# Two token tiles at a time between the layers, and key transposes one step later

## The chip, the cores and the metric

The kernel runs on one core of a Trainium2 chip. The metric is the device time of one execution in microseconds; lower is better. The kernel before takes 1199.09 us, the median of 3 runs (1197.3 to 1199.76).

## What is computed

Two layers of a hybrid encoder work on 512 tokens of 1024 features. Each layer makes one large input projection of the modulated input u, feeds two attention mixers with it, merges them through gates, projects back, adds the residual and normalises. The output of the first layer's normalisation is the second layer's input.

```
def hybrid_layer(x, c, ...):
    mod = jax.nn.silu(c) @ w_ada + b_ada
    shift, scale, gate = jnp.split(mod, 3, axis=-1)
    u = x * (1.0 + scale[:, None, :]) + shift[:, None, :]
    proj = u @ w_in
    aq, ak, av, az, bq, bk, bv, bz, gl = jnp.split(proj, SPLIT_POINTS, axis=-1)
    y_a = mixer_a(aq, ak, av, rel_table) * jax.nn.silu(az)
    y_b = mixer_b(bq, bk, bv, q_norm_g, k_norm_g) * jax.nn.silu(bz)
    g_a, g_b = jnp.split(jax.nn.sigmoid(gl + b_gate), 2, axis=-1)
    merged = g_a * (y_a @ w_pa) + g_b * (y_b @ w_pb)
    out = merged @ w_o
    return layer_norm(DEEPNORM_ALPHA * x + gate[:, None, :] * out, ln_g, ln_b)
```

Mixer B normalises queries and keys per head by their root mean square and rotates them before the scores; it uses 8 query heads (`bq`) and 2 key and value heads (`bk`, `bv`).

## The kernel before

**Number format.** Every large product is made of three TensorE products: each operand is held as a rounded high part and a low part, the difference. For u these are `uh` and `ul`, for weights `wh` and `wl` (or tiles `g` where the weights are kept longer). A weight chunk of 1024 x 256 comes in as two raw loads and is split in four pieces of two feature blocks each: ACT copies the high part (line 175), DVE subtracts for the low part (line 176).

**Order.** The order of each engine's instructions is the order in which the code is written out; each engine runs its own instructions in that order and waits on the others through semaphores. The program advances in ticks. `tick(n)` splits n weight pieces and runs what `later(k, f)` has put off by k ticks. With `split_first` the pieces come ahead of what was put off.

**Between the layers.** `out_proj` goes through 16 units, one for each column chunk j of 256 and token tile r of 128; a unit is 24 products of 256 columns, and DVE then empties it with three instructions (gate, residual, statistics; lines 1211, 1213, 1217). The last eight units are chunks 2 and 3 of tile 0, then of tile 1, 2 and 3. After chunk 3 of a tile, `layer_norm` takes the aggregate (line 1236), POOL raises to the power -1/2 (line 1238), and `normalise` refines that on DVE (lines 1244 to 1269) and scales the tile on ACT in two halves (line 1271). `make_u` transposes half a tile, four blocks of 128 x 128, on TensorE (line 944), ACT scales and shifts each block out of PSUM (line 948), makes `uh` (line 952), and DVE makes `ul` (line 953). `normalise` is put off by one tick, the two halves of `make_u` by `LN` = 2 and 3 ticks.

**The first chunks of layer 1.** `first_chunks` computes, for each token tile, one unit of keys and values (`bkv`, into the PSUM tile L) and one of the first queries (`bq0`, into T), and then four units of `bq1`. `FIRST` holds how many weight pieces are split after each unit.

**Steps of mixer B.** `b_steps` is a generator of small steps: rotate the keys, scale them (`k_scale`), take square sums and roots of queries (`q_sums`), transpose the keys (`b_keys`, line 597, copied out at 599 and 600) and rotate queries (`q_rotate`, lines 492 and 501). In layer 0 the last steps, in layer 1 those that are left, are run by `b_prepare`, with one unit of projection work between two of them (`weave`); then `mixer_b` transposes the first queries (line 613), takes their scores into L and their exponentials (line 637). POOL takes the roots of the square sums (line 480). Line 423 copies a row of the bias table out of PSUM.

Of the kernel before, what the change touches and what calls it, by code (L numbers as in the profile page):

```python
# [30 lines left out]
WARM = (6, 6)  # L31
AGE = 2
PIECES = (1, 1, 1, 1, 2, 2, 2, 2, 1, 1, 1, 1, 0, 0, 1, 1)
FIRST = (2, 1, 1, 1, 1, 0, 0, 1)
LN = (2, 3)


@with_exitstack
def trunk_kernel(ctx, tc, x, c, rel_table, ln_g, ln_b, w_ada, b_ada, w_in, b_gate,
# [41 lines left out]
    B1 = Slots(psum, "b", 4, [128, 512])  # L81
# [62 lines left out]
    hi_lo = {}  # L144
# [14 lines left out]
    def drop(key):  # L159
        for w in hi_lo.pop(key):  # L160
            if isinstance(w, Held):
                G.put(*w.tiles)
# [371 lines left out]
    def k_scale(st):  # L534

        v, y, t = (st["kn"][:, j] for j in range(3))
        newton(v, y, t)
        for rp in range(2):
            kd = st["kd", rp] = G.get()
            kdv = kd.rearrange("p (r h e d) -> p r h e d", r=2, h=2, e=2)  # L540
            for r2 in range(2):
                r = 2 * rp + r2
                dve.tensor_tensor(out=kdv[:, r2], in0=st["km"][:, r, :, None, :].to_broadcast([128, 2, 2, 64]),
                                  in1=y[:, 2 * r:2 * r + 2][:, :, None, None].to_broadcast([128, 2, 2, 64]), op=MUL)

    def q_sums(st, ch, rp):
        if "qn" not in st:
            st["qn"] = small.tile([128, 3, 32], F32, tag="qn", name=fresh("qn"))
        at = 16 * ch + 8 * rp
        square_sums(st["xq", ch, rp], st["qn"][:, 0, at:at + 8])  # L550
        first_root(st["qn"][:, 0, at:at + 8], st["qn"][:, 1, at:at + 8])
# [11 lines left out]
    def b_steps(st):  # L563

        k_rotate(st)
        yield
        k_scale(st)
        q_sums(st, 0, 0)
        yield
        b_keys(st)  # L570
        q_rotate(st, 0, 0)
        yield
        q_sums(st, 0, 1)
        q_sums(st, 1, 0)
        yield
        while ("xq", 1, 1) not in st:
            yield
        q_sums(st, 1, 1)
# [358 lines left out]

    xs = dsc.tile([512, 1024], F32, name="xs")

    def make_u(r, h, xn):  # L940

        b = B1.get()
        for k in range(4):
            pe.transpose(b[:, 128 * k:128 * k + 128], xn[:, 128 * k:128 * k + 128], idn)
        u = G.get()
        for k in range(4):
            kt, ks = 4 * h + k, slice(128 * k, 128 * k + 128)
            act.activation(u[:, ks], b[:, ks], AF.Identity, bias=aff[:, kt:kt + 1], scale=aff[:, 8 + kt:9 + kt])  # L948
        B1.put(b)
        uv = u.rearrange("p (k t) -> p k t", k=4)  # L950
        ks, ts = slice(4 * h, 4 * h + 4), slice(128 * r, 128 * r + 128)
        act.activation(uh[:, ks, ts], uv, AF.Copy)
        dve.tensor_sub(ul[:, ks, ts], uv, uh[:, ks, ts].bitcast(F32))
        G.put(u)

    def first_chunks(l, st):

        big_o = {"bkv": big("L"), "bq0": big("T")}

        def unit(n, r):  # L960
            token_mms(hi_lo[l, n], big_o[n][:, 256 * r:256 * r + 256], slice(128 * r, 128 * r + 128))
            if r % 2:
                o = big_o[n].rearrange("p (r n) -> p r n", r=4)[:, r - 1:r + 1]
                if n == "bkv":
                    b_copy_kv(r - 1, 2, o, st)
                else:
                    b_copy_q(0, r // 2, o, st)

        for r in range(4):
            for i, n in enumerate(("bkv", "bq0")):  # L970
                unit(n, r)
                if r == 3:
                    next(st["steps"], None)
                tick(FIRST[2 * r + i], True)
        drop((l, "bkv"))
        drop((l, "bq0"))
        for _ in token_chunk((l, "bq1"), lambda r: slice(128 * r, 128 * r + 128),
                             lambda rp, o: b_copy_q(1, rp, o.rearrange("p (r n) -> p r n", r=2), st)):
            next(st["steps"], None)

    def warm(o, n):

        for _ in range(n):
# [245 lines left out]
        for j in range(4):  # L1229
            drop((l, f"wo{j}"))  # L1230

    def layer_norm(l, r, xt, rows, bn):

        mv = small.tile([128, 6], F32, tag="mv", bufs=4, name=fresh("mv"))
        mean, v, y, t, nb = (mv[:, i:i + 1] for i in (0, 2, 3, 4, 5))
        dve.bn_aggr(mv[:, 0:2], bn.rearrange("p a b -> p (a b)"))
        dve.tensor_scalar(v, mv[:, 1:2], eps, None, op0=ADD)
        pool.tensor_tensor(out=y, in0=v, in1=mhalf, op=OP.pow)

        def put_out(h):  # L1240
            sp.dma_start(dram(out, r * 128 * D + 512 * h, [[D, 128], [1, 512]]), xt[h])

        def rstd():
            dve.scalar_tensor_tensor(t, y, v, y, op0=MUL, op1=MUL)
            dve.tensor_scalar(t, t, -0.5, 1.5, op0=MUL, op1=ADD)
            dve.tensor_mul(y, y, t)

        last = l == DEPTH - 1
        if last:
            def centre():  # L1250
                for h in range(2):
                    dve.scalar_tensor_tensor(xt[h], xt[h], mean, rows[0][h], op0=SUB, op1=MUL)  # L1252
                rstd()

            def finish():
                centre()
                for h in range(2):
                    dve.scalar_tensor_tensor(xt[h], xt[h], y, rows[1][h], op0=MUL, op1=ADD)  # L1258
                    put_out(h)

            if r == 3:
                run_later(True)
                finish()
            else:
                later(1, finish)
            return
        def normalise():
            rstd()
            dve.scalar_tensor_tensor(nb, mean, -1.0, y, op0=MUL, op1=MUL)
            for h in range(2):  # L1270
                act.activation(xt[h], xt[h], AF.Identity, scale=y, bias=nb)  # L1271

        later(1, normalise)
        for h in range(2):
            later(LN[h], lambda h=h: make_u(r, h, xt[h]))


    def row_tiles(src, offs):
# [7 lines left out]
    for l in range(DEPTH):  # L1286
        st = {"more": deque()}
        st["steps"] = b_steps(st)
        if l == 0:
            start_layer0(st)  # L1290
        else:
            todo = deque([(r, h) for r in range(4) for h in range(2)])

            def keep():
                if todo:
                    r, h = todo.popleft()
                    t = nxt[r][h]
                    dve.tensor_mul(t, t, gb[0][h])
                    dve.tensor_add(t, t, gb[1][h])
                    sp.dma_start(xs[128 * r:128 * r + 128, 512 * h:512 * h + 512], t)  # L1300
                    G.put(t)
                    if not todo:
                        G.put(*gb[0], *gb[1])

            first_chunks(l, st)
        yb = {n: G.get() for n in range(4)}
        ya, zs, merged, b_done = {}, {}, {}, {}
        src = x[0] if l == 0 else xs
        xt = {}

        def preload(n):
            for r in range(len(xt), min(len(xt) + n, 4)):
                xt[r] = [G.get(), G.get()]
                for h in range(2):
                    sp.dma_start(xt[r][h], src[128 * r:128 * r + 128, 512 * h:512 * h + 512])

        def main():
            yield from b_prepare(st, deque([keep] * 8 if l else []))
            yield from mixer_b(st, yb)
            b_done["b"] = True  # L1320
            G.put(st["v"], st["ks", 0], st["ks", 1])
            yield from mixer_a(st, 0, ya, deque([lambda: None] * 4 + [lambda: load_bias(st, 1)]))
            yield from mixer_a(st, 1, ya)

        def fill():
            yield from half_chunks(l, st, 0)
            yield from half_chunks(l, st, 1)
            yield from z_chunks(l, zs)
            yield from merge_chunks(l, ya, yb, b_done, zs, merged, preload)

        weave(main(), fill(), RATE)
        if l + 1 < DEPTH:
            rope_loads(l + 1)
            later(2, lambda: rope_tables(l + 1))
            later(1, lambda: affine(l + 1))
        preload(4)
        if l + 1 < DEPTH:
            rows = None
            gb = row_tiles(ln_g[l], [0]) + row_tiles(ln_b[l], [0])
        else:  # L1340
            rows = row_tiles(ln_g[l], [0]) + row_tiles(ln_b[l], [0])
        out_proj(l, merged, xt, lambda r, bn: layer_norm(l, r, xt[r], rows, bn))
        for t in merged.values():
            G.put(*t)
        if l + 1 < DEPTH:
            for hh in range(2):
                gate_tile(l + 1, hh)
        nxt = xt
# [49 lines left out]
```

## Time and profile before

| what | us |
|---|---|
| median of 3 runs | 1199.09 |
| profiled execution | 1199.13 |
| its span | 1197.0 |
| TensorE busy in the span | 1163.0 |
| DVE busy | 675.4 |
| ACT busy | 531.1 |
| POOL busy | 54.0 |

The span is the time from the first to the last instruction of the program that the profiler saw; the execution's own time has a little around it. Busy time is a union: a matmul's record is longer than the distance to the next one, so the start distances, not the lengths, give what a product costs. TensorE is the engine whose share decides; the others matter where TensorE waits for them.

### The profile page before, as it was taken

Reading aid. Unit: us, or ns where it says so; the run is one execution under the profiler, and the core shown is the slowest. Engines: PE = TensorE matmul, PEld = TensorE weight load, DVE = VectorE, ACT = ScalarE, POOL = GpSimd, SP = SyncE. Lnnn points to the kernel's source line nnn. Section 1 sums busy time; section 2 is a strip of 40 time slices with the busy share of each in tenths; the row PEclk is TensorE's granted clock in tenths of the full one; section 3 lists DMA queues with packets and bytes.
Section 4 is the critical chain, followed back from the end, with each engine's and each line's share of the span. In section 5 each row is a group of like instructions: output and inputs, shape, how many; then the busy total and the mean of one; then the engine's idle time right before and its main releaser. Section 6 shows DMA issues by size and latency. Waiting matters only on the chain.

```text
span 1197.0 us, 19187 instructions
## 1 busy us (share of the span) xinstructions
PE 1163.0 (97%) x7491; PEld 998.2 (83%) x7491; DVE 675.4 (56%) x1582; ACT 531.1 (44%) x1112; POOL 54.0 (5%) x85
## 2 busy tenths in 40 slices
PE   7899999999999999999989999999999999999996
PEld 6888888888887787888989888888878778888896
DVE  6776766655455365336755667664333533843477
ACT  2364544444554454323275545544554553533320
POOL 0021000001000000000002001000000000000000
PEclk9999999999999999999999999999999999999998
DMA  9935433546343243334522326335232223323331
GB/s 280 294 116 150 123 109 117 150 133 185 103 128 120 59 129 96 90 104 150 170 71 71 114 91 182 112 107 167 83 114 85 88 73 114 116 88 106 123 107 71
DMA packets 161314, 146.31 MB, mean 122 GB/s; under 512 B 8942, under 2 KB 149078, under 8 KB 161224
## 3 DMA queue, kind: packets, MB, share of 16 engines
q1 hardware_dynamic: 159176, 139.71, 38.5%
q0 software_dynamic: 2048, 5.38, 1.9%
q8 instruction: 59, 0.97, 0.3%
q14 instruction: 31, 0.25, 0.1%
HBM read 134.87 MB, written 8.62 MB: 120 GB/s over the span
## 4 chain that ended last, share of the span: by engine, by line
PE 88%; DVE 6%; ACT 2%; DMA 1%; issue 1%; SPq 1%; POOL 0%; DVEq 0%; ACTq 0%
PE b L90 75%; PE L L90 6%; PE T L663 5%; DVE acc L283 1%; PE T L90 1%; DMA raw<-in_w_ada_dram 1%; PE b L613 1%; DVE wl L176 1%; ACT g L948 0%; DMA s<-in_w_in_dram 0%; SPq L999 0%; DVE g L1252 0%; DVE g L1258 0%; ACT g L1271 0%; DVE wl L1023 0%
## 5 line engine op out<-in xcount | busy, mean ns | idle before, releaser
L176 DVE TENSOR_TENSOR wl<-raw,wh 128x512 fp32r<-128x512 f32 x304 | 205.1, 687 | 286.1 <-ACT wh L175 286.1
L90 PE MATMUL b<-uh,wh 128*128 128x512 f32 x768 | 308.4, 402 | 0.6 <-ACT g L423 0.6
L90 PE MATMUL b<-uh,wl 128*128 128x512 f32 x768 | 299.5, 390 | 1.7 <-DVE wl L176 1.7
L90 PE MATMUL b<-ul,wh 128*128 128x512 f32 x768 | 300.0, 391 | 0.0
L175 ACT ACTIVATE wh<-raw 128x512 fp32r<-128x512 f32 x304 | 179.9, 622 | 32.7 <-issue 24.8
L90 PEld LDWEIGHTS b<-uh,wh 128*128 128x128 f32 x768 | 144.0, 188 | 43.6 <-issue 12.0
L90 PEld LDWEIGHTS b<-uh,wl 128*128 128x128 f32 x768 | 144.2, 188 | 33.8 <-DVE wl L176 2.5
L90 PEld LDWEIGHTS b<-ul,wh 128*128 128x128 f32 x768 | 144.3, 188 | 27.6
L90 PE MATMUL b<-wh,uh 128*128 128x256 f32 x416 | 120.8, 290 | 0.0
L90 PE MATMUL b<-wl,uh 128*128 128x256 f32 x416 | 117.7, 283 | 0.0
L90 PE MATMUL b<-wh,ul 128*128 128x256 f32 x416 | 117.6, 283 | 0.0
L665 ACT ACTIVATE pt<-T 128x1024 f32<-128x1024 f32 x64 | 65.4, 1022 | 73.3 <-PE T L663 70.3
L738 ACT ACTIVATE s<-s,ast 128x256 f32<-128x256 f32 x128 | 63.5, 497 | 68.3 <-DVE ast L733 62.9
L283 DVE SCALAR_TENSOR_TENSOR acc<-raw,sc,acc 128x256 f32<-128x256 f32 x168 | 81.3, 484 | 8.4 <-DMA raw<-in_w_ada_dram 3.2
L90 PEld LDWEIGHTS b<-wh,uh 128*128 128x128 f32 x416 | 79.5, 191 | 4.8 <-issue 3.6
L90 PEld LDWEIGHTS b<-wl,uh 128*128 128x128 f32 x416 | 79.5, 191 | 0.8 <-DVE wl L176 0.2
L90 PEld LDWEIGHTS b<-wh,ul 128*128 128x128 f32 x416 | 79.4, 191 | 0.0
L90 PE MATMUL b<-g,wh 128*128 128x512 f32 x256 | 79.2, 391 | 0.0
L637 ACT ACTIVATE s<-L,bst,qn 128x512 f32<-128x512 f32 x64 | 49.2, 773 | 65.9 <-DVE bst L634 65.9
L90 PE MATMUL b<-wh,g 128*128 128x256 f32 x384 | 71.4, 284 | 0.7 <-DVE g L1191 0.5
L90 PE MATMUL b<-pt,g 128*64 128x128 f32 x1024 | 70.0, 279 | 0.0
L90 PEld LDWEIGHTS b<-pt,g 128*64 128x64 f32 x1024 | 54.6, 136 | 17.7 <-issue 13.7
(177 smaller groups left out, 1615.5 us busy)
## 6 DMA issues: line engine op xcount, KB each, us to landing
raw<-in_w_in_dram SPq DMA_DIRECT2D x126, 512.0 KB, 4.1
raw<-in_w_ada_dram SPq DMA_DIRECT2D x96, 256.0 KB, 3.9
raw<-in_w_o_dram SPq DMA_DIRECT2D x16, 512.0 KB
g<-in_x_dram SPq DMA_DIRECT2D x16, 256.0 KB, 5.5
vph<-g SPq DMA_DIRECT2D x16, 256.0 KB, 2.1
g<-vph SPq DMA_DIRECT2D x16, 256.0 KB, 6.0
g<-frow SPq DMA_DIRECT2D x32, 128.0 KB, 3.1
raw<-in_w_pa_dram SPq DMA_DIRECT2D x8, 512.0 KB, 3.5
```

Source lines behind the costliest of these rows:

```text
L90: pe.matmul(o, l, r, start=start, stop=stop, skip_group_check=True)
L175: act.activation(hi[:, d], raw[:, s], AF.Copy)
L176: dve.tensor_sub(lo[:, d], raw[:, s], hi[:, d].bitcast(F32))
L283: dve.scalar_tensor_tensor(a, raw[:, k], col, a, op0=MUL, op1=ADD)
L613: pe.transpose(o[:, 128 * e:128 * e + 128], qd[:, 2 * (hp % 2) + e], idn)
L637: act.activation(p[:, 512 * e:512 * e + 512], lg[:, 512 * e:512 * e + 512], AF.Exp, scale=f[:, e:e + 1], bias=sm[:, 0, e:e + 1], accum_out ...
L663: pe.transpose(t[:, 128 * j:128 * j + 128], p[:, 128 * j:128 * j + 128], idn)
L665: act.activation(pt, t, AF.Copy)
L738: act.activation(p4[:, e, b], p4[:, e, b], AF.Exp, bias=sm[:, e, b:b + 1], accum_out=s_t[:, rb, e, 1:2])
```

## The change

Four edits. The normalisation of a tile between the layers is issued in the same tick as its statistics, no longer one tick later. `make_u` takes two token tiles and a quarter of the features in place of one tile and half of them: its four transposes are followed by two scaled copies of 256 columns in place of four of 128. Nothing is made until the second tile of a pair is normalised; two of the four pieces are then made two ticks later, and two three ticks later. The first chunks go through tiles 0 and 1 for `bkv`, `bq0` and `bq1` and then through tiles 2 and 3, with another list of weight pieces, and the steps of mixer B advance only after units of tile 3. In `b_steps` scaling the keys and the first square sums are two steps, and the last three square sums are one.

```
--- before.py
+++ after.py
@@ -31,8 +31,9 @@
 WARM = (6, 6)
 AGE = 2
 PIECES = (1, 1, 1, 1, 2, 2, 2, 2, 1, 1, 1, 1, 0, 0, 1, 1)
-FIRST = (2, 1, 1, 1, 1, 0, 0, 1)
-LN = (2, 3)
+FIRST = (("bkv", 0, 2), ("bq0", 0, 1), ("bkv", 1, 1), ("bq0", 1, 2), ("bq1", 0, 0), ("bq1", 1, 0),
+         ("bkv", 2, 0), ("bq0", 2, 0), ("bkv", 3, 1), ("bq0", 3, 2), ("bq1", 2, 1), ("bq1", 3, 1))
+LN = (2, 2, 3, 3)
 
 
 @with_exitstack
@@ -565,6 +566,7 @@
         k_rotate(st)
         yield
         k_scale(st)
+        yield
         q_sums(st, 0, 0)
         yield
         b_keys(st)
@@ -572,7 +574,6 @@
         yield
         q_sums(st, 0, 1)
         q_sums(st, 1, 0)
-        yield
         while ("xq", 1, 1) not in st:
             yield
         q_sums(st, 1, 1)
@@ -937,18 +938,20 @@
 
     xs = dsc.tile([512, 1024], F32, name="xs")
 
-    def make_u(r, h, xn):
+    def make_u(r, j, xt):
 
         b = B1.get()
-        for k in range(4):
-            pe.transpose(b[:, 128 * k:128 * k + 128], xn[:, 128 * k:128 * k + 128], idn)
+        for k in range(2):
+            for i in range(2):
+                c = 128 * (2 * (j % 2) + k)
+                pe.transpose(b[:, 256 * k + 128 * i:256 * k + 128 * i + 128], xt[r + i][j // 2][:, c:c + 128], idn)
         u = G.get()
-        for k in range(4):
-            kt, ks = 4 * h + k, slice(128 * k, 128 * k + 128)
+        for k in range(2):
+            kt, ks = 2 * j + k, slice(256 * k, 256 * k + 256)
             act.activation(u[:, ks], b[:, ks], AF.Identity, bias=aff[:, kt:kt + 1], scale=aff[:, 8 + kt:9 + kt])
         B1.put(b)
-        uv = u.rearrange("p (k t) -> p k t", k=4)
-        ks, ts = slice(4 * h, 4 * h + 4), slice(128 * r, 128 * r + 128)
+        uv = u.rearrange("p (k t) -> p k t", k=2)
+        ks, ts = slice(2 * j, 2 * j + 2), slice(128 * r, 128 * r + 256)
         act.activation(uh[:, ks, ts], uv, AF.Copy)
         dve.tensor_sub(ul[:, ks, ts], uv, uh[:, ks, ts].bitcast(F32))
         G.put(u)
@@ -966,18 +969,26 @@
                 else:
                     b_copy_q(0, r // 2, o, st)
 
-        for r in range(4):
-            for i, n in enumerate(("bkv", "bq0")):
+        o1 = {}
+
+        def last(r):
+            if r % 2 == 0:
+                o1[0] = B1.get()
+            o = o1[0]
+            token_mms(hi_lo[l, "bq1"], o[:, 256 * (r % 2):256 * (r % 2) + 256], slice(128 * r, 128 * r + 128))
+            if r % 2:
+                b_copy_q(1, r // 2, o.rearrange("p (r n) -> p r n", r=2), st)
+                B1.put(o)
+
+        for n, r, k in FIRST:
+            if n == "bq1":
+                last(r)
+            else:
                 unit(n, r)
-                if r == 3:
-                    next(st["steps"], None)
-                tick(FIRST[2 * r + i], True)
-        drop((l, "bkv"))
-        drop((l, "bq0"))
-        for _ in token_chunk((l, "bq1"), lambda r: slice(128 * r, 128 * r + 128),
-                             lambda rp, o: b_copy_q(1, rp, o.rearrange("p (r n) -> p r n", r=2), st)):
-            next(st["steps"], None)
-
+            if r == 3:
+                next(st["steps"], None)
+                drop((l, n))
+            tick(k, True)
     def warm(o, n):
 
         for _ in range(n):
@@ -1229,8 +1240,9 @@
         for j in range(4):
             drop((l, f"wo{j}"))
 
-    def layer_norm(l, r, xt, rows, bn):
-
+    def layer_norm(l, r, tiles, rows, bn):
+
+        xt = tiles[r]
         mv = small.tile([128, 6], F32, tag="mv", bufs=4, name=fresh("mv"))
         mean, v, y, t, nb = (mv[:, i:i + 1] for i in (0, 2, 3, 4, 5))
         dve.bn_aggr(mv[:, 0:2], bn.rearrange("p a b -> p (a b)"))
@@ -1270,9 +1282,10 @@
             for h in range(2):
                 act.activation(xt[h], xt[h], AF.Identity, scale=y, bias=nb)
 
-        later(1, normalise)
-        for h in range(2):
-            later(LN[h], lambda h=h: make_u(r, h, xt[h]))
+        normalise()
+        if r % 2:
+            for j, n in enumerate(LN):
+                later(n, lambda j=j: make_u(r - 1, j, tiles))
 
 
     def row_tiles(src, offs):
@@ -1339,7 +1352,7 @@
             gb = row_tiles(ln_g[l], [0]) + row_tiles(ln_b[l], [0])
         else:
             rows = row_tiles(ln_g[l], [0]) + row_tiles(ln_b[l], [0])
-        out_proj(l, merged, xt, lambda r, bn: layer_norm(l, r, xt[r], rows, bn))
+        out_proj(l, merged, xt, lambda r, bn: layer_norm(l, r, xt, rows, bn))
         for t in merged.values():
             G.put(*t)
         if l + 1 < DEPTH:
```

The order of ACT's instructions between the layers. Line 1271 (1283 after) normalises a tile, 948 and 952 (951 and 955) make u and its high part, 175 (176) copies weight pieces; raw_5515 and raw_5558 are the halves of the `bq0` chunk. Before, from the normalisation of tile 2 on:

```order
L1271 ACTIVATE g_5280<-g_5280,mv_5839 128x512
L1271 ACTIVATE g_5281<-g_5281,mv_5839 128x512
L175 ACTIVATE wh_5872<-raw_5515 128x512
L948 ACTIVATE g_5932<-b_5927,aff 128x128 x4
L952 ACTIVATE uh<-g_5932 128x4x128
L175 ACTIVATE wh_5872<-raw_5558 128x512 x2
L948 ACTIVATE g_5984<-b_5979,aff 128x128 x4
L952 ACTIVATE uh<-g_5984 128x4x128
L1271 ACTIVATE g_5284<-g_5284,mv_5939 128x512
L1271 ACTIVATE g_5285<-g_5285,mv_5939 128x512
```

After, from the same normalisation on:

```order
L1283 ACTIVATE g_5280<-g_5280,mv_5823 128x512
L1283 ACTIVATE g_5281<-g_5281,mv_5823 128x512
L176 ACTIVATE wh_5862<-raw_5515 128x512
L951 ACTIVATE g_5871<-b_5866,aff 128x256 x2
L955 ACTIVATE uh<-g_5871 128x2x256
L951 ACTIVATE g_5881<-b_5876,aff 128x256 x2
L955 ACTIVATE uh<-g_5881 128x2x256
L176 ACTIVATE wh_5862<-raw_5515 128x512
L1283 ACTIVATE g_5284<-g_5284,mv_5919 128x512
L1283 ACTIVATE g_5285<-g_5285,mv_5919 128x512
L176 ACTIVATE wh_5862<-raw_5558 128x512 x2
```

The two pieces of raw_5558 stood ahead of the last normalisation and now stand behind it.

The order of DVE's instructions around the statistics of tile 2 (tile g_5281 is its second half; 1236 and 1248 aggregate; 1211 to 1217 and 1222 to 1228 empty a unit). Before:

```order
L1211 TENSOR_TENSOR wot_5823<-b_5798,gate_631 128x256
L1213 SCALAR_TENSOR_TENSOR g_5281<-g_5281,wot_5823 128x256
L1217 BN_STATS bn_5407<-g_5281 128x6
L953 TENSOR_TENSOR ul<-g_5832,uh 128x4x128
L1236 BN_AGGR mv_5839<-bn_5407 128x2
L1237 TENSOR_SCALAR mv_5839<-mv_5839 128x1
L1211 TENSOR_TENSOR wot_5868<-b_5843,gate_631 128x256
L1213 SCALAR_TENSOR_TENSOR g_5285<-g_5285,wot_5868 128x256
L1217 BN_STATS bn_5439<-g_5285 128x6
```

After:

```order
L1222 TENSOR_TENSOR wot_5799<-b_5774,gate_631 128x256
L1224 SCALAR_TENSOR_TENSOR g_5281<-g_5281,wot_5799 128x256
L1228 BN_STATS bn_5407<-g_5281 128x6
L956 TENSOR_TENSOR ul<-g_5808,uh 128x2x256
L956 TENSOR_TENSOR ul<-g_5818,uh 128x2x256
L1248 BN_AGGR mv_5823<-bn_5407 128x2
L1249 TENSOR_SCALAR mv_5823<-mv_5823 128x1
L1256 SCALAR_TENSOR_TENSOR mv_5823<-mv_5823 128x1
```

Before, the aggregate followed the low part of one piece of tile 1; now it follows those of two pieces of tiles 0 and 1 together.

The order of ACT's instructions in layer 0 from the first key copies (line 599, 600 after) to the first query copies (615, 616). Line 898 (899) copies out a unit of the projection, 475 (476) squares queries, 489 (490) swaps halves for the rotation. Before:

```order
L599 ACTIVATE g_834<-b_829 128x512
L599 ACTIVATE g_842<-b_837 128x512
L489 ACTIVATE s_845<-g_772 128x16x16 x2
L898 ACTIVATE g_878<-b_800 128x512
L175 ACTIVATE wh_825<-raw_623 128x512
L475 ACTIVATE s_885<-g_776 128x512
L475 ACTIVATE s_890<-g_774 128x512
L175 ACTIVATE wh_825<-raw_625 128x512
L475 ACTIVATE s_922<-g_778 128x512
L615 ACTIVATE qst_930<-b_927 128x256
L615 ACTIVATE qst_936<-b_933 128x256
```

After:

```order
L899 ACTIVATE g_853<-b_794 128x512
L176 ACTIVATE wh_819<-raw_623 128x512
L600 ACTIVATE g_865<-b_860 128x512
L600 ACTIVATE g_873<-b_868 128x512
L490 ACTIVATE s_876<-g_772 128x16x16 x2
L176 ACTIVATE wh_819<-raw_625 128x512
L476 ACTIVATE s_912<-g_776 128x512
L476 ACTIVATE s_917<-g_774 128x512
L476 ACTIVATE s_922<-g_778 128x512
L616 ACTIVATE qst_930<-b_927 128x256
L616 ACTIVATE qst_936<-b_933 128x256
```

Before, the copy of a projection unit stands between the key copies and the query copies; now it stands ahead of both, and three squares follow each other.

## Rows read from the trace of the kernel before

**Rows 1.** The page, busy us (share of the span) and instructions by engine.

```profile
PE 1163.0 (97%) x7491; PEld 998.2 (83%) x7491; DVE 675.4 (56%) x1582; ACT 531.1 (44%) x1112; POOL 54.0 (5%) x85
```

**Rows 2.** Groups by shape, TensorE: busy us, mean ns | idle before, releaser.

```profile
L944 PE MATMUL b<-idn,g 128*128 128x128 f32 x32 | 5.1, 282 | 6.0 <-ACT g L1271 6.0
...
L597 PE MATMUL b<-idn,g 128*128 128x128 f32 x16 | 3.5, 299 | 0.3 <-DVE g L543 0.3
```

**Rows 3.** Timeline of TensorE between the layers: start, length, what, idle before.

```profile
592.98 3.04 PE L90 MATMUL b<-g,g 128*128 128x256 f32 x24
596.72 0.66 PE L944 MATMUL b<-idn,g 128*128 128x128 f32 x4 [0.71 <-ACT g L1271]
...
622.47 0.74 PE L944 MATMUL b<-idn,g 128*128 128x128 f32 x4 [1.82 <-ACT g L1271]
...
623.23 0.42 PE L90 MATMUL L<-wl,uh 128*128 128x256 f32 x1
623.44 0.41 PE L90 MATMUL L<-wh,ul 128*128 128x256 f32 x1
```

**Rows 4.** Windows: length, busy of PE, PEld, DVE, ACT, POOL, granted clock, DMA.

```profile
623.00:626.20 3.20, 3.20 (x17) 3.20 (x16) 1.17 (x2) 2.66 (x7) 0.00 (x0) 0.50 0.03 9
```

**Rows 5.** Timeline of ACT between the layers.

```profile
595.86 1.52 ACT L1271 ACTIVATE g<-g,mv 128x512 f32<-128x512 f32 x2 [9.65 <-DVE mv L1269]
...
599.32 0.63 ACT L952 ACTIVATE uh<-g 128x512 fp32r<-128x512 f32 x1
...
616.95 1.14 ACT L175 ACTIVATE wh<-raw 128x512 fp32r<-128x512 f32 x2
...
621.61 1.52 ACT L1271 ACTIVATE g<-g,mv 128x512 f32<-128x512 f32 x2 [1.47 <-DVE mv L1269]
```

**Rows 6.** Timeline of DVE between the layers.

```profile
592.15 0.26 DVE L1236 BATCH_NORM_AGGREGATE mv<-bn 128x2 f32<-128x24 f32 x1
...
595.03 0.21 DVE L1244 SCALAR_TENSOR_TENSOR mv<-mv 128x1 f32<-128x1 f32 x1
...
595.66 0.16 DVE L1269 SCALAR_TENSOR_TENSOR mv<-mv 128x1 f32<-128x1 f32 x1
...
599.98 0.69 DVE L953 TENSOR_TENSOR ul<-g,uh 128x512 fp32r<-128x512 f32 x1 [1.35 <-ACT uh L952]
...
604.24 0.42 DVE L1211 TENSOR_TENSOR wot<-b,gate 128x256 f32<-128x256 f32 x1
...
605.15 0.43 DVE L1217 BATCH_NORM_STATS2 bn<-g 128x6 f32<-128x256 f32 x1
```

**Rows 7.** Timeline of POOL between the layers.

```profile
592.68 0.57 POOL L1238 TENSOR_TENSOR mv<-mv,mhalf 128x1 f32<-128x1 f32 x1 [24.07 <-DVE mv L1237]
```

**Rows 8.** Lines 948 and 1034 alone: duration ns min/median/max, first and last start, forms.

```profile
L948 ACT ACTIVATE g<-b,aff x32: 438/451/482, 597.8 to 629.6; 128x128 f32<-128x128 f32 x32
...
L1034 ACT ACTIVATE g<-b,mod x8: 778/778/783, 12.1 to 56.7; 128x512 f32<-128x512 f32 x8
```

**Rows 9.** Timeline of TensorE in layer 0, keys and first queries.

```profile
68.07 1.77 PE L597 MATMUL b<-idn,g 128*128 128x128 f32 x8 [0.25 <-DVE g L543]
...
75.43 0.60 PE L613 MATMUL b<-idn,g 128*128 128x128 f32 x4
...
87.69 0.50 PE L90 MATMUL b<-uh,wh 128*128 128x512 f32 x1 [0.60 <-ACT g L423]
```

**Rows 10.** Timeline of DVE in layer 0, rotation of the first queries.

```profile
73.11 1.29 DVE L501 TENSOR_TENSOR g<-g,s 128x512 f32<-128x512 f32 x2
```

**Rows 11.** Timeline of POOL in layer 0, roots of the query sums.

```profile
75.88 4.83 POOL L480 TENSOR_TENSOR qn<-qn,mhalf 128x8 f32<-128x8 f32 x3 [3.93 <-DVE qn L479]
```

**Rows 12.** Timeline of TensorE in layer 1, the same transposes.

```profile
645.05 1.74 PE L597 MATMUL b<-idn,g 128*128 128x128 f32 x8
...
655.26 0.60 PE L613 MATMUL b<-idn,g 128*128 128x128 f32 x4
```

**Rows 13.** Timeline of DVE in layer 1, rotation of the first queries.

```profile
650.69 1.29 DVE L501 TENSOR_TENSOR g<-g,s 128x512 f32<-128x512 f32 x2
```

## The prediction, made before the changed kernel ran

> **What bounds the kernel now.** I read the page's busy line first: TensorE is busy for 1163.0 of 1197.0 us [rows 1], so an edit is worth what it does to TensorE's waits or its clock, and nothing else. The groups of TensorE instructions by shape say where it waits: the 32 transposes of line 944, between the layers, lost 6.0 us, all to ACT's normalisation at line 1271, and the 16 key transposes of line 597 a little to DVE [rows 2]. TensorE's timeline shows the first of the four waits between the layers, 0.71 us, and the last, 1.82 us [rows 3]. It also gives the unit of this stage: 24 products of 256 columns, whose starts reach over 3.04 − 0.28 + 0.12 = 2.88 us, 0.120 us each. After the fourth wait the products start 0.21 us apart, and the stretch that follows has a granted clock of 0.50, which is the 1.2 GHz level [rows 3, 4]. About 15 products there take 0.21 instead of 0.12 and the transposes ahead of them stretch too: 1.45 us. Those 7.4 us are all that the boundary can give. I then read ACT, DVE and POOL over the same stretch to see what each wait hangs on [rows 5 to 7].
>
> The profiled execution took 1199.13 us with a span of 1197.0; the median of the runs is 1199.09. I add to the former; the 0.04 between them does not matter.
>
> **Part 1, between the layers: the waits removed.** Normalisation of a token tile used to be queued one unit late, behind another unit's three DVE instructions. At once, it is ready in time for its transposes, which now come two units later. The four waits go: −6.0 us.
>
> **Part 1: what is late next.** I play the new order from the end of the unit of column chunk 3 and tile 1, called (3,1), at 592.98 + 2.88 = 595.9 [rows 3]. TensorE, unhindered: units (2,2) and (3,2) to 601.6; eight transposes of 0.109 (0.87) to 602.5; unit (2,3) to 605.4; eight transposes to 606.2; unit (3,3) to 609.1. Then the first `bkv` unit may start.
>
> ACT must by then have made u for tiles 0 and 1, in four pieces of 512 columns: two scaled copies of 256 columns and one rounding copy (0.63 [rows 5]) each. No row shows the scaled copy at 256 columns; at 128 it takes 0.451 and at 512 0.778 [rows 8], and these are my bounds. I take 0.56, the straight line between them, since both are the same operation from the same memory. The Trainium skill (ScalarE: Activation LUTs, What ACT_TABLE_LOAD costs) gives 0.28 us for a column pointer as bias, 0.09 for the second pointer and 0.833 ns an element, which is an estimate of 0.585; by that the sum would be 0.3 higher. A piece thus costs ACT about 1.5 with overlaps. Pieces 0 and 1 are rounded at 605.2 and DVE has their low parts 0.69 later [rows 6], 605.9.
>
> Only now does DVE reach the statistics of tile 2, which stand behind those low parts. From the aggregate to the normalisation: 0.53 to POOL's root, 0.57 there, 0.79 for the four small DVE instructions, some 0.06 between [rows 6, 7]: 1.95. ACT waits at the normalisation until 607.9, takes 1.52 for its two halves [rows 5], then a weight piece (0.5), then pieces 2 and 3: rounded at 611.5 and 613.0, low parts at 612.2 and 613.7. The `bkv` unit begins at 609.1, does 12 products on pieces 0 and 1, and waits twice; it ends at 614.2 instead of 612.0. **+2.2.**
>
> Tile 3 is behind that. DVE empties its last unit only after the low part at 613.7: three instructions from the row at 604.24 to the end of that at 605.15, 1.34; a weight piece 0.6; the chain 1.95: normalisation starts at 617.6 and ends at 619.1. Behind it on ACT stand weight pieces 2 and 3 of `bq0`. Before, they ran at 616.95, ahead of the fourth normalisation (621.61) [rows 5]; now they follow it. They are rounded at 619.8 and 620.3, their low parts done at 620.4 and 621.0. The first `bq0` unit starts at 614.2, loses 0.6 to its second piece, has done 12 products by 616.2, waits 3.5 and again 0.6, and ends at 621.7 instead of 617.1. **+4.6.**
>
> In rows 5 ACT idles 9.65 and 1.47 ahead of two normalisations, for DVE; no row shows whether it could have taken another instruction in that time. The Trainium skill (Perfetto Trace Analysis, Tensor Engine Instruction) calls ACT's and DVE's queues strictly first in, first out, which speaks against the new order: by it the 3.5 stands in full, and if weight pieces could overtake a waiting normalisation it would be gone, with a sum of +2.4.
>
> The first `bq1` unit, now third instead of after `bq0`, needs its weight pieces 2 and 3, which stand on ACT behind the second pair's u: 0.2 and 0.6. **+0.8.** Added 7.6, removed 6.0: **+1.6** at full clock. A wait of over 3.5 us close behind shorter ones should bring the 1.2 GHz stretch back at least once, where waits of up to 1.82 did [rows 3, 4]: 1.45 before, 1.45 after, ±0 (bounds −1.45 and +1.5).
>
> **Part 2, key transposes one step later, in both layers.** The keys are scaled earlier than they are transposed, so the eight transposes no longer wait: layer 0 took from 68.07 to 69.6, 1.5 for 0.87 [rows 9], −0.6 in each layer. But the query rotation is issued with them, and the step in which the query transposes (line 613) follow is the next one now: one unit lies between, not two. From the first key transpose at 68.07 to the first rotated tile at 73.11 + 0.69 = 73.8 [rows 9, 10] are 5.7, less the 0.6: 5.1. Before, TensorE had transposes and two units in between, the query transposes at 75.43 came after that, and nothing showed. Now it has 0.87 + 2.88 = 3.75. The wait is **+1.4** in layer 0. In layer 1 the same stretch is 645.05 to 650.69 + 0.69, 6.3 less 0.6, and another square sum and weight piece stand on the queues: 5.9 − 3.75, **+2.1**. Before, the query transposes came at 655.26 [rows 12, 13].
>
> Right behind, three square sums are now issued together and DVE does them ahead of the low part of the transposed queries, on which the scores wait: **+0.4** in each layer. POOL's three roots take 4.83 us [rows 11]. Before, they ended at 75.88 + 4.83 = 80.7, 5.3 after the query transposes. Now, from the first rotated tile on, DVE has 0.6 for the second, 0.6 for a weight piece and 0.9 for a square sum before POOL can start: 2.1 + 4.83 = 6.9. That is 1.6 later, 0.4 of it counted already, and what follows (exponentials, the copies that free PSUM tiles) moves with it. In layer 0 TensorE already waits there, 0.60 on ACT's line 423 [rows 9]: **+1.2**. In layer 1 no wait is in the rows of before; I take nothing, and keep 1.2 for the range.
>
> Layer 0: 1.4 + 0.4 + 1.2 − 0.6 = **+2.4**. Layer 1: 2.1 + 0.4 − 0.6 = **+1.9**.
>
> **Costed at nothing.** The same 32 transposes; half as many scaled copies, on ACT, whose waiting decides and not its work; DMA issues, the same in number, on a queue that TensorE was not waiting for; the later mixers one step further behind the projections, where TensorE's groups show no wait worth a term. If that cover fails it costs some tenths.
>
> Sum: 1.6 + 0 + 2.4 + 1.9 = +5.9; 1199.13 + 5.9 = **1205.0 us**.
>
> **The rivals.**
> (B) The clock falls for two stretches instead of one, since the waits in `bkv` and in `bq0` are both longer than 1.82: +1.5, 1206.5. For it: one stretch followed a wait of 1.82 [rows 3, 4]. Against it: time at half clock costs nothing while TensorE waits.
>
> (C) The `bq0` pieces are not late, because ACT reaches the fourth normalisation sooner than I count (scaled copies near 0.45, DVE emptying tile 3 earlier). Then 3.5 + 0.6 of the added 7.6 goes, and with no long wait the slow stretch too: 5.9 − 4.1 − 1.45 = +0.35, 1199.5, no change. For it: pieces 2 and 3 need only some 3 us. Against it: each of the chain's steps has a row.
>
> (D) The boundary runs without a wait, and the change is faster. The place is tile 2's normalisation on ACT. If it is over before pieces 0 and 1 are, nothing on ACT stands behind a wait, and `bkv` and `bq0` find their operands. It decides whether the statistics of tile 2 are done by some 602, ahead of the low parts, or at 607.9. Then −6.0 − 1.45, and part 2's +4.3 remain: −3.15, 1196.0. Against it: DVE's order puts them behind; for it only that TensorE ended that tile's last unit at 601.6.
>
> **How the numbers follow.** Forecast A 0.64, B 0.20, C 0.10, D 0.06. A's own range is 1202.0 to 1208.0: the scaled copy at 0.45 instead of 0.56 takes off about 1.3, at 0.78 adds 2.6; the clock −1.45; layer 1's roots +1.2. For 8 in 10, 1200.6 to 1208.4, which leaves out C, D and the far ends. A measurement of this kernel tells about 0.2% (2.4 us) from no change. Faster takes D and a little of C, 0.07; same takes the rest of C and A's low edge, 0.11; slower 0.82.
>
> **What would show it.** In the changed profile the transposes between the layers wait for nothing. TensorE waits inside the first `bkv` unit for ACT and DVE of u, for 3 us or so inside the first `bq0` unit for the weight copies of line 176, with ACT idle ahead of the fourth normalisation. The query transposes show 1.4 and 2.1 us behind DVE's rotation, the key transposes nothing. I am wrong if `bq0` runs without a break, or if the query transposes follow their unit at once.

## The result, and the profile after

The changed kernel takes 1206.8 us (median of 4 runs, 1206.19 to 1207.44) against 1199.12 (4 runs, one more than in the table above): a ratio of 1.0070, 95% interval 1.0055 to 1.0084. The forecast was 1205.0, in a range from 1200.6 to 1208.4. The profiled execution took 1206.19 us with a span of 1204.4, 7.4 more than before, and that is what there is to account for. Three of the runs below hold one execution that is far longer at a lower granted clock; it is left out of their times and ratios.

The groups of TensorE instructions by shape, between 590 and 700 us, answer to [rows 2] (busy us, mean ns | idle before, releaser):

```profile
L947 PE MATMUL b<-idn,g 128*128 128x128 f32 x32 | 4.5, 289 | 0.0
L614 PE MATMUL b<-idn,g 128*128 128x128 f32 x10 | 2.2, 334 | 2.5 <-DVE g L502 2.5
L598 PE MATMUL b<-idn,g 128*128 128x128 f32 x8 | 1.0, 272 | 0.0
```

The transposes between the layers and the key transposes wait for nothing, as forecast; the query transposes now do. TensorE's timeline between the layers answers to [rows 3] (start, length, what, idle before):

```profile
595.45 3.04 PE L91 MATMUL b<-g,g 128*128 128x256 f32 x24
...
611.57 0.28 PE L91 MATMUL L<-wh,uh 128*128 128x256 f32 x1
...
614.23 0.39 PE L91 MATMUL L<-wh,uh 128*128 128x256 f32 x1 [1.06 <-ACT uh L955]
...
617.55 0.41 PE L91 MATMUL T<-wh,uh 128*128 128x256 f32 x1
617.76 0.41 PE L91 MATMUL T<-wl,uh 128*128 128x256 f32 x1
...
622.25 0.38 PE L91 MATMUL T<-wh,uh 128*128 128x256 f32 x1 [2.27 <-ACT wh L176]
622.98 0.58 PE L91 MATMUL T<-wl,uh 128*128 128x256 f32 x1 [0.34 <-DVE wl L177]
...
625.50 1.42 PE L947 MATMUL b<-idn,g 128*128 128x128 f32 x8
...
635.21 0.38 PE L91 MATMUL b<-g,uh 128*128 128x256 f32 x1 [0.24 <-ACT g L176]
635.93 0.39 PE L91 MATMUL b<-g,uh 128*128 128x256 f32 x1 [0.34 <-DVE g L177]
```

The first `bkv` unit reaches from 611.57 to 617.55, 5.98 in place of 2.88; the first `bq0` unit from 617.55 to 625.50, 7.95 in place of 2.88. The two waits in `bq1` are there too. ACT's timeline over the same stretch answers to [rows 5] and shows what the two units wait for:

```profile
610.56 1.52 ACT L1283 ACTIVATE g<-g,mv 128x512 f32<-128x512 f32 x2 [2.58 <-DVE mv L1281]
611.99 0.61 ACT L176 ACTIVATE wh<-raw 128x512 fp32r<-128x512 f32 x1
612.51 1.00 ACT L951 ACTIVATE g<-b,aff 128x256 f32<-128x256 f32 x2
...
615.65 0.61 ACT L176 ACTIVATE wh<-raw 128x512 fp32r<-128x512 f32 x1
620.16 1.52 ACT L1283 ACTIVATE g<-g,mv 128x512 f32<-128x512 f32 x2 [3.90 <-DVE mv L1281]
621.59 1.13 ACT L176 ACTIVATE wh<-raw 128x512 fp32r<-128x512 f32 x2
```

ACT idles 2.58 us ahead of the third normalisation with pieces of u behind it, and 3.90 ahead of the fourth with the two weight pieces behind it that TensorE needs at 619.8.

The windows with a low granted clock (length, busy of PE, PEld, DVE, ACT, POOL, granted clock, DMA) are three where [rows 4] has one:

```profile
616.50:619.50 3.00, 2.97 (x14) 2.98 (x15) 2.24 (x7) 0.00 (x0) 0.54 (x1) 0.51 0.02 4
623.30:626.60 3.30, 3.30 (x18) 3.30 (x18) 0.83 (x2) 0.08 (x1) 0.00 (x0) 0.55 0.47 156
664.00:667.30 3.30, 3.30 (x17) 3.30 (x18) 3.20 (x8) 1.81 (x4) 1.49 (x1) 0.51 0.35 86
```

The third follows the query transposes of layer 1. TensorE's timeline in layer 0 and then in layer 1 answers to [rows 9, 12]:

```profile
70.76 1.03 PE L598 MATMUL b<-idn,g 128*128 128x128 f32 x8
...
76.32 0.63 PE L614 MATMUL b<-idn,g 128*128 128x128 f32 x4 [1.65 <-DVE g L502]
...
80.28 0.96 PE L91 MATMUL L<-g,qst 128*128 128x512 f32 x3 [0.23 <-DVE qst L617]
...
90.17 0.50 PE L91 MATMUL b<-uh,wh 128*128 128x512 f32 x1 [1.65 <-ACT g L424]
...
657.50 1.03 PE L598 MATMUL b<-idn,g 128*128 128x128 f32 x8
...
663.87 1.08 PE L614 MATMUL b<-idn,g 128*128 128x128 f32 x4 [2.47 <-DVE g L502]
```

**Where the 7.4 us are.** Unit (3,1) starts at 595.45, before at 592.98 [rows 3]: +2.5 up to the end of layer 0. From there to the key transposes of layer 1 it was 52.07 [rows 3, 12] and is 62.05; three units more lie in between now, as the steps advance only after units of tile 3, so 62.05 − 8.64 − 52.07 = +1.3 for the boundary. The rest of 7.4, +3.6, is layer 1, and counted wait by wait it is 3.4: the query transposes could have begun at 657.50 + 0.87 + 2.88 = 661.25, came 2.6 later, and the 1.2 GHz stretch behind them takes some 1.5; the key transposes give back 0.7, since they reach over 0.79 and no longer over 1.50 [rows 12].

### The profile page after: what moved, and what is told of

It reads as the page before. It is cut to its first block, busy times and chain, and to the rows that moved or that the text cites. A ratio compares the mean times of both kernels' runs of the same rounds, so it can differ in the third digit from the quotient of the medians.

```text
span 1204.4 us, 19167 instructions
## 1 busy us (share of the span) xinstructions
PE 1166.4 (97%) x7491; PEld 1001.0 (83%) x7491; DVE 675.8 (56%) x1582; ACT 526.7 (44%) x1096; POOL 52.5 (4%) x85
## 4 chain that ended last, share of the span: by engine, by line
PE 87%; DVE 7%; ACT 2%; DMA 2%; SPq 1%; issue 1%; POOL 1%; DVEq 0%; ACTq 0%
PE b L91 74%; PE L L91 6%; PE T L664 5%; DVE acc L284 1%; DMA g<-in_x_dram 1%; PE T L91 1%; DVE wl L177 1%; SPq L1010 1%; PE b L614 1%; ACT g L951 0%; DMA s<-in_w_in_dram 0%; DVE g L1264 0%; DVE g L1270 0%; POOL qn L481 0%; DMA raw<-in_w_in_dram 0%
```

## The experiments

Each ratio is to runs of the kernel before on the same chip, whose median was 1198.2 to 1198.7.

**The three edits apart and in pairs.** The change has three parts that can be put in alone: pairs with the new order of the first chunks, normalisation at once, and the steps.

Steps as before, in the changed kernel:

```
-        k_scale(st)
-        yield
-        q_sums(st, 0, 0)
+        k_scale(st)
+        q_sums(st, 0, 0)
...
         q_sums(st, 1, 0)
+        yield
         while ("xq", 1, 1) not in st:
```

> The changed kernel with the steps of mixer B as before (keys scaled and transposed at the old distance, the last three square sums not together). My theory: the 2.4 us of layer 0 go, and in layer 1 the wait of 2.5 us at the query transposes with its slow stretch of 1.4 goes, but since the steps still advance only after units of tile 3, waits of about 0.9 and 1.0 stay there: about 1206.8 - 2.4 - 2.0 = 1202.4. Rival: the steps cost only layer 0 and the rest of the loss lies between the layers: 1204.4, with the wait in layer 1 as in the changed kernel.

Measured 1202.51, ratio 1.0037 (1.0025 to 1.0049), as my theory had it. The waits of TensorE (engine, line, waited for: us, times, longest) say what stays without the new steps: the first two are in layer 1, the third is the old one of layer 0.

```profile
PE b L614 <- DVE g L502: 0.9, 1, 0.9
PE L L91 <- DVE qst L617: 0.8, 1, 0.8
PE b L91 <- ACT g L424: 0.6, 1, 0.6
```

The steps alone, in the kernel before (the same edit the other way):

> The kernel before with nothing changed but the steps of mixer B. My prediction booked +2.4 in layer 0 and +1.9 in layer 1 on the steps: 1203.4. Rival: layer 1's wait comes from the new order of the first chunks, in which the steps advance three times and not six; the steps alone then cost only layer 0: 1201.5, and no wait at the query transposes of layer 1.

Measured 1199.0, ratio 1.0008 (1.0000 to 1.0017), lower than either number. Its waits:

```profile
PE b L944 <- ACT g L1271: 5.9, 4, 1.8
...
PE b L613 <- DVE g L501: 1.7, 1, 1.7
PE b L90 <- ACT g L423: 1.6, 1, 1.6
```

The query transposes wait once, in layer 0, and not in layer 1. So the rival was right on the place: the wait in layer 1 needs the new order of the first chunks (which comes with the pairs). Both theories missed the total: the waits of layer 0 are there in full, but the stretch at 1.2 GHz is absent, which gives back some 1.45. The four waits are the same; this is the window behind the fourth, where [rows 4] has 0.50:

```profile
624.80:628.80 4.00, 3.97 (x34) 3.97 (x35) 1.38 (x2) 3.62 (x9) 0.00 (x0) 1.00 0.05 14
```

Normalisation one tick later, in the changed kernel:

```
-        normalise()
+        later(1, normalise)
```

> The changed kernel with the normalisation put off by one tick again; pairs, order of the first chunks and steps stay. My theory: what costs is that the normalisations stand on ACT ahead of pieces that are needed sooner; put off, the second and third normalisation let u of tiles 0 and 1 and the weight pieces of the first queries pass, the 3.1 us in the first bkv unit and most of the 5.1 in the first bq0 unit go, about 2.8 us of short waits stay or come: 1200 (1199 to 1202). Rival: normalising at once is what removed the four waits of 6.0 us; put off, the transposes wait for it again: 1207 or more.

Measured 1198.79, ratio 1.0005 (0.9997 to 1.0014): 0.65% below the changed kernel by one word. No wait of [rows 2] comes back in full, and none is left in the first `bkv` unit; the four waits that belong to this place are

```profile
PE b L91 <- ACT g L176: 0.5, 1, 0.5
PE b L947 <- ACT g L1283: 0.5, 1, 0.5
...
PE T L91 <- DVE wl L177: 0.3, 1, 0.3
PE b L91 <- DVE g L177: 0.3, 1, 0.3
```

and from 612 to 626 us the granted clock is 1.00:

```profile
612.00:626.00 14.00, 13.15 (x105) 12.31 (x104) 7.86 (x21) 10.70 (x20) 0.94 (x1) 1.00 0.36 114
```

In layer 1 the query transposes wait as long as in the changed kernel, and yet the granted clock stays at 1.00 behind them. The timeline, then the window:

```profile
651.05 1.03 PE L598 MATMUL b<-idn,g 128*128 128x128 f32 x8
...
657.42 0.63 PE L614 MATMUL b<-idn,g 128*128 128x128 f32 x4 [2.47 <-DVE g L502]
```

```profile
655.00:665.00 10.00, 7.35 (x56) 6.93 (x57) 7.74 (x19) 3.43 (x7) 5.36 (x4) 1.00 0.30 85
```

So not all of the 0.65% is the place of the normalisation. Of the 7.5 us between the two profiled executions 6.2 lie between the key transposes of layer 0 (at 70.51 here) and those of layer 1. Behind these 1.1 are saved, where the one difference that shows is the absent stretch.

Normalisation at once alone, in the kernel before (the same edit the other way):

> The kernel before with nothing changed but that normalisation is issued at once. My theory: three of the four waits at the transposes go (about 1.3 us is left of 6.0), but the two weight pieces of the first queries fall behind the fourth normalisation here too, and the first bq0 unit waits about 1.3, 4.0 and 0.6: 1199.6 to 1201, no gain. Rival: at once is a gain by itself and only the pairs lose it: 1199.1 - 4.7 = 1194.4.

Measured 1200.11, ratio 1.0016 (1.0007 to 1.0025), as my theory had it. TensorE's timeline: one wait at the transposes is left, and the first `bq0` unit takes over.

```profile
611.42 0.66 PE L944 MATMUL b<-idn,g 128*128 128x128 f32 x4 [1.14 <-ACT g L1271]
...
617.27 0.38 PE L90 MATMUL T<-wl,uh 128*128 128x256 f32 x1 [1.05 <-DVE wl L176]
621.89 0.58 PE L90 MATMUL T<-wh,uh 128*128 128x256 f32 x1 [3.76 <-ACT wh L175]
```

Pairs and the new order alone (both edits above together):

> Pairs of token tiles and the new order of the first chunks alone: normalisation one tick later and the steps of mixer B as before. If the parts add: 1198.8 (normalisation late) less the 4.3 that the old steps gave back in the changed kernel, 1194.5, with waits of 0.9 and 0.8 at the first queries of layer 1 and some 2.8 us of short waits between the layers. Rival: the two savings overlap (one slow stretch saved twice), 1196 to 1197.

Measured 1195.84, ratio 0.9977 (0.9968 to 0.9986): faster than before, and between my two numbers. The parts in the order of their ratios: pairs alone 0.9977, steps alone 1.0008, at once alone 1.0016, pairs and steps 1.0005, pairs and at once 1.0037, all three 1.0070. At once costs 1.9 us alone and about 7 beside the pairs; the steps cost 1.0 alone and 3.4 beside the pairs. For the first the waits give the reason: at once alone takes 4.9 of the 6.0 us from the transposes between the layers (1.14 is left), but with the pairs only 0.5 is there to be taken, so that what it makes late stands alone. In the second the clock has a share, since the run with the steps alone shows no 1.2 GHz stretch.

**Is it the place in ACT's queue?** Normalisation stays at once; the two weight pieces go ahead of the fourth one, and u of tiles 2 and 3 one tick later.

```
-PIECES = (..., 0, 0, 1, 1)
-FIRST = (("bkv", 0, 2), ...
+PIECES = (..., 0, 0, 1, 3)
+FIRST = (("bkv", 0, 0), ...
...
-            for j, n in enumerate(LN):
+            for j, n in enumerate(LN if r == 1 else (3, 3, 4, 4)):
```

> The changed kernel with normalisation at once as it is, but weight pieces 2 and 3 of the first queries split after the last unit of the output projection, so ahead of the fourth normalisation on ACT, and u of tiles 2 and 3 one tick later so that its transposes don't wait for that normalisation. My theory (the pieces are late only because they stand behind the fourth normalisation): the 2.3 and 0.3 us inside the first bq0 unit, its slow products and the 1.1 us in the first bq1 unit go, the 3.1 in the first bkv unit and the steps' costs stay: 1206.8 - 5.5 = 1201.3 (1200.5 to 1202.5). Rival: ACT has no room there, and the lost time only turns up at other operands: 1205 or more.

Measured 1199.57, ratio 1.0010 (1.0001 to 1.0019): more came back than I expected, and the rival is out. ACT's timeline:

```profile
615.18 1.66 ACT L176 ACTIVATE wh<-raw 128x512 fp32r<-128x512 f32 x3
620.90 1.53 ACT L1283 ACTIVATE g<-g,mv 128x512 f32<-128x512 f32 x2 [4.06 <-DVE mv L1281]
```

ACT idles ahead of the fourth normalisation for as long as in the changed kernel, but nothing that TensorE needs soon stands behind it: `bq0` has one wait of 0.28 left, and neither 1.2 GHz stretch between the layers is there. The later u of tiles 2 and 3 was not tried apart from the early pieces.

**Would earlier statistics have freed the boundary (case D)?**

```
             unit(j, r)
-            tick(...)
             if j == 3:
                 done(r, bn[r])
+            tick(...)
...
-LN = (2, 2, 3, 3)
+LN = (3, 3, 4, 4)
```

> The changed kernel with each tile's statistics and normalisation issued ahead of the tick that follows its last unit, so on DVE ahead of the low parts and on ACT ahead of u (the pieces of u come at the same ticks as in the changed kernel). By my prediction's case D the boundary then runs without a wait: 1206.8 - 9.5 = 1197. My theory now: a normalisation early on ACT only stands longer ahead of what is needed first; the pieces of u for tiles 0 and 1 and weight pieces 2 and 3 wait behind the second and the fourth, and the transposes for PSUM tiles: 1209 to 1211.

Measured 1209.95, ratio 1.0097 (1.0080 to 1.0114). The normalisation stands earlier in the queues, but it does not come sooner. DVE in the changed kernel, then in this run; line 1248 is the aggregate of tile 2:

```profile
608.63 0.26 DVE L1248 BATCH_NORM_AGGREGATE mv<-bn 128x2 f32<-128x24 f32 x1
```

```profile
606.62 0.69 DVE L177 TENSOR_TENSOR wl<-raw,wh 128x512 fp32r<-128x512 f32 x1 [2.11 <-ACT wh L176]
...
609.85 0.26 DVE L1248 BATCH_NORM_AGGREGATE mv<-bn 128x2 f32<-128x24 f32 x1
```

Unit (3,1) starts 0.57 later here, so the aggregate is 0.65 later and not earlier. On ACT the weight copy now stands behind the normalisation of tile 1; the low part at 606.62 waits for that copy, and what empties the next two units waits behind the low part, ahead of the aggregate. Case D's condition, statistics of tile 2 by some 602, did not come about. TensorE waits for the weight pieces, and for PSUM tiles that ACT and DVE empty later:

```profile
PE T L91 <- ACT wh L176: 3.6, 1, 3.6
...
PE b L947 <- ACT g L951: 1.5, 1, 1.5
PE b L91 <- DVE wot L1222: 1.3, 1, 1.3
```

**What brings the clock down?** Throwaway products where TensorE waits:

```
             if kt == 4:
+                for _ in range(fill):
+                    mm(d[:, 0:128], idn, ones, True, True)
...
```

> The changed kernel with throwaway products of 128 columns put where TensorE waits: 2 ahead of the third piece in the first bkv unit, 5 ahead of it in the first bq0 unit, 5 ahead of the query transposes of layer 1. They fit into the waits and delay nothing. If idling is what brings the clock down to 1.2 GHz, the three stretches with a granted clock near 0.5 go and the time falls by 3 to 4 us, to 1203. If the clock falls for another reason, the stretches stay and the time is 1206.8 or a little more.

Measured 1204.98, ratio 1.0052 (1.0036 to 1.0067): the first and the third stretch were gone. One remained, behind the wait that was left 1.92 us long, so this run alone settled nothing.

> As the run with throwaway products, with twice as many (4, 10 and 10), since one took only 0.24 us and the ten columns pairs in the longest wait left 1.9 us of it idle. If idling brings the clock down, the last stretch (623.8 to 627.3, where 1.9 us stayed idle) goes too: 1205.3 - 1.4 = 1203.9. If not, a stretch with a granted clock near 0.5 is still there.

Measured 1203.52, ratio 1.0045 (1.0030 to 1.0060). The three windows that answer to those of the changed kernel:

```profile
616.30:619.30 3.00, 2.73 (x22) 2.52 (x22) 2.21 (x8) 0.00 (x0) 0.54 (x1) 1.00 0.12 11
621.80:625.10 3.30, 2.92 (x23) 2.72 (x23) 1.90 (x3) 1.51 (x4) 0.00 (x0) 1.00 0.40 115
661.80:665.10 3.30, 3.22 (x27) 3.23 (x28) 3.23 (x8) 1.81 (x4) 1.19 (x1) 1.00 0.26 41
```

The operands came no sooner: the third piece was there 2.64 us after the start of the `bkv` unit (2.66 in the changed kernel), the weights of `bq0` 10.67 after it (10.68), the rotated queries 6.28 after the first key transpose (6.37). The span is 2.9 us shorter; 0.4 of it lies ahead of the key transposes of layer 0, where nothing was changed, so the low clock cost about 2.5 in the changed kernel. One execution without a stretch could be chance, but all four executions list a mean granted clock of 0.994 to 0.997 and the four of the changed kernel 0.990 to 0.993, and their times don't overlap.

**Which of the two edits to the steps costs in layer 0?** The key transposes stay one step later, the last square sum gets its own step again (`yield` ahead of `while`).

> The changed kernel, but the last square sum a step after the two others again; the key transposes stay one step later. My theory: the query transposes then have two units and wait in neither layer (in layer 1 the slow stretch of 1.4 goes too), but the roots come still later, and in layer 0 TensorE's wait on line 424 grows from 1.65 to some 3.6: 1206.8 + 1.1 in layer 0 - 2.3 - 1.4 in layer 1 = 1204.2. Rival: the three sums together are what costs in layer 0 (0.4 + 1.2 of its 2.4); apart, the wait on line 424 falls back to 0.6 and the time to 1206.8 - 4.0 - 3.7 + 1.4 = 1200.5.

Measured 1206.0, ratio 1.0071 (1.0054 to 1.0088). The query transposes wait in neither layer, as both expected. But the wait on line 424 grew, and in the profiled execution, the slowest of the three, a 1.2 GHz stretch came behind it, which I had not counted. Its row in the timeline, then the window:

```profile
90.25 0.79 PE L91 MATMUL b<-uh,wh 128*128 128x512 f32 x1 [3.27 <-ACT g L424]
```

```profile
90.20:94.20 4.00, 3.95 (x9) 3.13 (x10) 1.80 (x5) 1.52 (x3) 1.37 (x3) 0.50 0.29 66
```

The run with the steps as before differs from this one by that step alone, and waits 0.6 there. So it is the later step itself that costs, also where the last square sum stands apart.

**A version from all this.** Pairs; normalisation later for tiles 2 and 3 only; the pieces of `bq0` all ahead of the fourth; the steps of before, with one more unit ahead of the query transposes in layer 1.

```
-PIECES = (..., 0, 0, 1, 1)
+PIECES = (..., 0, 0, 2, 2)
-FIRST = (("bkv", 0, 2), ...
+FIRST = (("bkv", 0, 0), ...
...
         q_rotate(st, 0, 0)
         yield
+        if l:
+            yield
...
-        normalise()
+        if r > 1:
+            later(1, normalise)
+        else:
+            normalise()
...
+            for j, n in enumerate(LN if r == 1 else (3, 3, 4, 4)):
```

> What the runs so far point to: pairs, normalisation one tick later for tiles 2 and 3 only, the weight pieces of the first queries all split ahead of the fourth normalisation, u of tiles 2 and 3 one tick later, the steps as before with one more unit between the key transposes and the query transposes in layer 1. All the waits between the layers but some 0.4 us should go, and those of layer 1: 1199 - 6.0 - 1.4 + 0.4 - 0.6 = 1191.4 (1190 to 1193). If shorter queues elsewhere take the time back: 1195 or more.

Measured 1191.18, ratio 0.9939 (0.9925 to 0.9952): faster than both. One wait is left between the layers and up to the first queries of layer 1:

```profile
PE T L91 <- DVE wl L177: 0.3, 1, 0.3
```

## Why the prediction was right, step by step

**The waits removed** (−6.0): right in amount. The prediction put them down to normalising at once together with transposes two units later. Either part nearly does it alone (1.1 us is left with at once alone, 0.5 with the pairs alone), so beside the pairs at once gains 0.5 and not 6.0.

**What is late next** (+2.2, +4.6, +0.8): right in place and cause. With slow products in them, the first `bkv` unit ran over by 3.1 and the first `bq0` unit by 5.1. The scaled copy of 256 columns, set at 0.56, took 0.548 to 0.577. The prediction's estimate from the Trainium skill (ScalarE: Activation LUTs, What ACT_TABLE_LOAD costs) is 0.585; the measurement decides, and the straight line between the two rows was nearer. The third normalisation started at 610.56 and the fourth at 620.16, which after the 2.5 of layer 0 are 608.1 and 617.7; the prediction had 607.9 and 617.6. The 3.5 in `bq0` ends where it was forecast (622.25 less 2.5, against 619.8) but shows as 2.27: the unit began 0.9 later than forecast and the nine products ahead of the wait ran 0.21 apart, which took 0.8, while the 0.6 for its second piece did not come. That weight pieces don't pass a waiting normalisation, for which the Trainium skill was cited (Perfetto Trace Analysis, Tensor Engine Instruction), is what the trace shows with 3.90 us of idle time and what the run with early pieces shows from the other side.

**The clock at the boundary** (±0): right in the sum, wrong in the picture. Two stretches came, as in case B, but the first ended just ahead of the wait in `bq0`, which took up what it had cost; that is what the prediction held against B. The boundary as a whole is +1.3 against +1.6.

**Layer 0** (+2.4): measured +2.5 at the end of the layer. The query transposes waited 1.65 (forecast 1.4), the scores 0.23 (0.4), line 424 went from 0.60 to 1.65 (+1.05 for +1.2), the key transposes gave back 0.7 (0.6). These come to 2.2; 0.3 is not located.

**Layer 1** (+1.9): measured +3.6. This term was mis-sized, in three ways. The wait was 2.6 and not 2.1. The 0.4 for the scores does not show, since the products ahead of them are slow here; with the clock kept up (twice the throwaway products) it is 0.30. And the sentence on the clock spoke of the boundary alone, while here too a 1.2 GHz stretch followed the wait in this execution, 1.5 us; in the run with the normalisation late it did not follow the same wait. In the span the forecast was +5.9 and +7.4 was measured; this term is +1.7 of the difference, the others −0.2. It also had the cause wrong: I booked it on the steps, but the steps alone cost nothing in layer 1, the order of the first chunks alone leaves waits of 0.9 and 0.8, and only both together give 2.5.

**Case D** (1196.0) stays untested. The run that issues the statistics earlier took 1209.95, but its aggregate of tile 2 came later. What it shows is that an earlier place in the code does not bring the statistics early here, since the weight pieces then stand behind the normalisation.

**Costed at nothing**: nothing shows against it. The 2.5, 1.3 and 3.6 are the whole difference of the spans, and counted wait by wait the first and the last come to 2.2 and 3.4, so some 0.4 is not located.

What stays open: how the chip decides on the clock. After the same four waits it fell in the profiled execution of the kernel before and did not in that with the steps alone; after 2.47 us in layer 1 it fell in the changed kernel and did not in the run with the normalisation late. The kernel before itself seems to run with and without its stretch: beside four of the experiments ten of its 21 runs took 1197.3 to 1198.0 us at a mean granted clock of 0.995 to 0.997, the others 1198.7 to 1199.7 at 0.993 to 0.996. The forecast of +5.9 was added to an execution with a stretch.

## What to carry to other kernels

When an instruction is issued earlier on an engine that runs in order, look at what is queued behind it and not at who waits for it: here the same normalisation, one tick later, was worth 0.65%, most of it between the layers. A wait that an edit leaves behind may be paid twice, once as idle time and once in the products after it; allow for the slower clock at every place where the edit leaves a wait as long as those that have it in the trace, not only where it stands already, and allow for it as a range, since the same wait can go without. And price parts together: normalising at once costs 1.9 us alone, where its gain pays for most of what it makes late, and about 7 beside the pairs, which have that gain already.

## What was not expected of the hardware

A wait that is filled with useless products costs less than an idle one: with 24 of them, 4, 10 and 10, the three windows rose from a granted clock of 0.51 to 0.55 to 1.00, and the time fell from a ratio of 1.0070 to 1.0045 with every operand as late as before. And a slow stretch can be free: from 617.55 to 619.5 products ran 0.21 apart, and TensorE then waited 2.27 us for weights that would not have come sooner.
